# The low half of every second weight block in two mixers, formed by ScalarE and an accumulating DMA in place of a VectorE subtraction

## The chip, the cores and the metric

The kernel runs on one core of one Trainium2 chip. A time is microseconds (us) of device time for one execution of the whole program. The span is the time from the first to the last instruction of the one execution that the hardware profiler recorded.

## The reference

The model is two layers, each of a half-weighted SwiGLU feed-forward, a token mixer and a second feed-forward, with layer norms between; 256 tokens, width 1024, all in float32. The mixer projects `u` by one wide matrix and feeds three branches (a 31-tap causal depthwise convolution, a state-space block, an attention block), whose outputs are gated, merged and projected.

```python
def hybrid_token_mixer(u, w_in, ...):
    proj = jnp.einsum('bsd,de->bse', u, w_in)
    a_in, b_in, c_in, g_in = _split(proj, [A_IN, B_IN, C_IN, GATE_IN])
    y_a = conformer_conv(a_in, ...) @ w_a_out
    y_b = mamba2_ssd(b_in, ...) @ w_b_out
    y_c = nsa_attention(c_in, ...) @ w_c_out
    g = jax.nn.sigmoid(g_in)...
    merged = g[:, :, 0] * y_a + g[:, :, 1] * y_b + g[:, :, 2] * y_c
    return merged @ w_o
```

## The kernel before

**Weights.** The weights come as 128x128 tiles, eight to a unit of 512 KB (`unit`). One DMA on SP's queue loads a unit into a `raw` buffer. For most matrices a float32 product is made of three fast matmuls: ScalarE (ACT) rounds the unit into `whi` (type fp32r), VectorE (DVE) subtracts to get `wlo = raw - whi`, and TensorE (PE) multiplies whi by xh, wlo by xh and whi by xl (`triple`, three lines of code, so three matmuls a tile and 24 a unit). There are 6 buffers for raw, 4 for whi and 4 for wlo, handed out in the order of the units.

**Order.** Every operation is first recorded with a cost, a key (the number of the weight tile at which it is wanted) and its buffers. `schedule` then plays the engines forward with these costs and writes each engine's instructions in the order that comes out. So a changed operation changes the order of all that follows, and the engines then run their lists strictly in order. An operation's `slow` is the time that the planner allows between its end and its users.

**The mixer**, in the order of its keys: `early` and `mix_v` (first projections), `mix_small`, `mix_a` (projection for the convolution, 12 units; the taps themselves are DVE instructions `ca<-ap` and `acc<-ap`, spread with keys up to 670 tiles later), `mix_c` (keys and queries, 16 units), `gates("g2")`, `mix_x` and `attend` (state-space inputs and attention), `merge(0)`, then `mix_z`, `gates("g1")`, `merge(1)` with the `ssd` steps among them, `gates("g0")`, `conv_end`, `merge(2)` (8 units in each of the five) and `mix_out`. At the head of the attention stands `attend_cmp`, run twice: scores `cs` on PE, `st` on ACT, transposes `ct` on PE, a softmax on DVE (`cmx`, `ce`, `csm`), transposes `cp` on PE, `pct` on ACT, and a product `ob`. POOL does small memsets only (`S`, `ap`, `xp`, `kcz`).

Of the kernel before, what the change touches and what calls it, by code (L numbers as in the profile page):

```python
# [13 lines left out]
AF = mybir.ActivationFunctionType  # L14
ALU = mybir.AluOpType
# [78 lines left out]
class Buf:  # L94


    def __init__(self, pool, tag, shape, dt, name, psum):
        self.pool, self.tag, self.shape, self.dt, self.name, self.psum = pool, tag, tuple(shape), dt, name, psum
        self.real = None
        self.live = False  # L100
        self.left = 0
        self.end = 0.0
        self.writes, self.reads = [], []
# [63 lines left out]
def real(x):  # L167
    return x.ap() if isinstance(x, View) else x
# [176 lines left out]
LOW = 0  # L345
# [6 lines left out]
TAIL = (62, 3.0, 44, 30, 4)  # L352
FRONT = 0
MOVE = 2.2
NRAW = 2
ADA0 = 200


class Net(Plan):
    BIG = 11  # L360
    TMP = 12
    RAW = 6
    WHI = 4
    WLO = 4
# [1 line left out]
    def __init__(self, ctx, tc, a):  # L366
        super().__init__()
        self.tc, self.nc, self.a = tc, tc.nc, a
        ctx.enter_context(tc.manual_schedule())
        pool = lambda name, bufs, **k: ctx.enter_context(tc.tile_pool(name=name, bufs=bufs, **k))  # L370
        self.pools = {
            "one": pool("one", 1), "raw": pool("raw", self.RAW), "whi": pool("whi", self.WHI), "wlo": pool("wlo", self.WLO),
            "pad": pool("pad", 1), "b8": pool("big", self.BIG), "t": pool("tmp", self.TMP), "m2": pool("m2", 2), "m3": pool("m3", 3), "m4": pool("m4", 4), "m8": pool("m8", 8),
            "mm": pool("ps", 2, space=PSUM), "x": pool("px", 6, space=PSUM)}
        self.slots = {"raw": self.RAW, "whi": self.WHI, "wlo": self.WLO, "b8": self.BIG, "t": self.TMP, "mm": 2, "x": 6}
        self.pools["pad"].tile([P, 48], F32, name="pad", tag="pad")
        self.nunit = a["ws"].shape[0]
        self.tile_no = 0
        self.keyed = None
        self.mod = {}  # L380
        self.modbuf = {}
        self.splits = {}
        self.last = []
# [140 lines left out]
    def move(self, *pairs):  # L524
# [3 lines left out]

        self.rec("DMA", 0.7 * len(pairs), fn, [p[0] for p in pairs], [p[1] for p in pairs], self.key(), slow=MOVE)

    def unit(self, u, native):
        raw = self.buf(self.pools["raw"], "raw", (P, UNIT * P), F32, "raw")
        base = u * UNIT
        src = self.a["ws"][u]
        self.dma(raw, src, P * UNIT * P * 4, key=base - LEAD)
        self.raw = raw
        if native:
            return
        for n in range(UNIT // SPLIT):
            s = raw[:, n * SPLIT * P:(n + 1) * SPLIT * P]  # L540
            k = base + n * SPLIT - self.EARLY
            hi = self.buf(self.pools["whi"], "whi", (P, SPLIT * P), F32R, "whi")
            lo = self.buf(self.pools["wlo"], "wlo", (P, SPLIT * P), F32R, "wlo")
            self.act(hi, s, AF.Copy, key=k)
            self.tt(lo, s, hi, ALU.subtract, key=k + LOW)
            self.splits[u * (UNIT // SPLIT) + n] = (hi, lo)

    EARLY = 20
# [396 lines left out]
    def mixer(self, l, ada=()):  # L945
        z = self.early(4)
        self.mix_v()
        self.mix_small()
        self.mix_a(l, z)
        self.mix_c(l)  # L950
        self.gates("g2")
        self.mix_x()
        self.attend()
        self.merge(0, self.oh_, self.ol_, th="g2")
        self.ssd0 = self.tile_no
        ada = list(ada)

        def side(i):
            for j in range(COUNT[i] if ada else 0):
                self.ada(*ada.pop(0), self.tile_no + 8 + STEP0 * j)  # L960

        side(0)
        self.mix_z()
        side(1)
        self.gates("g1")
        side(2)
        self.merge(1, *self.ssd(), th="g1")
        side(3)
        self.gates("g0")
        y = self.conv_end()  # L970
        side(4)
        self.merge(2, *y, th="g0")
        self.mix_out(l)

    def mix_v(self):
# [567 lines left out]
    def start(self):  # L1543
# [7 lines left out]
        def raw(k):  # L1551
            n = 2 * FIRST[0] * k - LEAD - FRONT
            raws.append(self.ada_raw(0, k, n))
            self.dma(self.x[:, k], self.a["x"][:, k], P * T * 4, n + 1)

        for k in range(NRAW):
            raw(k)

        def ready(k):
            if k + NRAW < KT:  # L1560
                raw(k + NRAW)
            self.ada(0, 8 + k, -100 + k, k, raws[k])
            self.ts(A[:, k:k + 1], self.mod[0][:, 8 + k:9 + k], 1.0, None, ALU.add, key=-100 + k)
            with self.at(-100 + k):
                self.u_tile(k, self.x[:, k], A[:, k:k + 1], self.mod[0][:, k:k + 1])
            if k == KT - 1:
                for d in range(KT):
                    self.act(self.ha[:, d], self.x[:, d], AF.Copy, scale=ALPHA, key=200)
# [175 lines left out]
```

## Time and profile before

| | |
|---|---|
| median of three runs | 1643.82 us (1637.28 to 1645.85) |
| the profiled execution's own time | 1638.38 us |
| its span | 1636.6 us |
| TensorE busy in the span | 1581.8 us (97%) |
| VectorE busy | 1380.3 us (84%) |
| ScalarE busy | 980.0 us (60%) |
| DMA queue of SP | 350.26 MB, 61.7% of 16 engines' span |

The median is the number that runs are compared by; the span and the stretches below are of the one profiled execution. "Busy" of TensorE includes the overlap of pipelined matmuls, so where it is 100% of a stretch the number of matmuls in that stretch says how fast they went.

### The profile page before, as it was taken

To read this page: it belongs to the slowest core of one execution; us is meant where nothing else is said; L and a number is where in the kernel's file an instruction comes from. 1 tells how busy PE (TensorE), PEld (TensorE's weight loads), DVE (VectorE), ACT (ScalarE), POOL (GpSimd) and SP (SyncE) were. 2 spreads that over 40 slices of the span, in tenths; PEclk is the share of its full clock that TensorE was granted. 3 is DMA by queue.
4 is the path that set the end of the run, shared out by engine and by line. 5 is a ranking of instruction groups with operands and counts; after the bars stand their busy time and mean duration, and the time that the engine had idled before them with its cause. 6 is when DMAs were issued, how large, how long until landed. Compare 5 with 4: busy or idle time off the path is not lost.

```text
span 1636.6 us, 33313 instructions
## 1 busy us (share of the span) xinstructions
PE 1581.8 (97%) x13224; PEld 1503.7 (92%) x13224; DVE 1380.3 (84%) x2675; ACT 980.0 (60%) x1809; POOL 8.3 (1%) x64
## 2 busy tenths in 40 slices
PE   6999999999999999999999999998999999999997
PEld 6999989889988888999989999997999899989996
DVE  7899789999999986899678885999999997776655
ACT  4744585578746466644474445845796567574443
POOL 0000000000000000000000000000000000000000
PEclk9999999999999999999999999999999999999998
DMA  9899665533276555899767985645332544557661
GB/s 375 328 342 406 211 216 179 173 130 100 80 280 206 182 175 188 291 359 361 249 232 272 345 296 174 232 158 172 118 107 91 180 155 165 191 186 234 229 198 46
DMA packets 89883, 352.37 MB, mean 215 GB/s; under 512 B 10368, under 2 KB 13696, under 8 KB 80000
## 3 DMA queue, kind: packets, MB, share of 16 engines
q1 hardware_dynamic: 89728, 350.26, 61.7%
q8 instruction: 103, 1.69, 0.4%
q14 instruction: 52, 0.43, 0.1%
HBM read 343.86 MB, written 1.05 MB: 211 GB/s over the span
## 4 chain that ended last, share of the span: by engine, by line
PE 86%; DVE 7%; DMA 3%; ACT 3%; issue 1%; SPq 0%; ACTq 0%; DVEq 0%
PE mm L573 16%; PE mm L574 16%; PE mm L575 16%; PE mm L451 3%; PE a L451 2%; PE a L589 2%; PE g L573 2%; PE g L574 2%; PE g L575 2%; PE xb L573 2%; DVE wlo L470 2%; PE xb L574 2%; PE xb L575 2%; PE sb L1069 2%; PE ob L1069 1%; DMA ada<-in_ada 1%
## 5 line engine op out<-in xcount | busy, mean ns | idle before, releaser
L507 ACT ACTIVATE whi<-raw 128x1024 fp32r<-128x1024 f32 x470 | 496.7, 1058 | 313.5 <-PE mm L575 147.0
L470 DVE TENSOR_TENSOR wlo<-raw,whi 128x1024 fp32r<-128x1024 f32 x470 | 572.3, 1220 | 130.6 <-ACT whi L507 128.8
L573 PE MATMUL mm<-uh,whi 128*128 128x256 f32 x1392 | 384.9, 277 | 0.9 <-DVE h L470 0.9
L574 PE MATMUL mm<-uh,wlo 128*128 128x256 f32 x1392 | 384.3, 276 | 0.0
L575 PE MATMUL mm<-ul,whi 128*128 128x256 f32 x1392 | 384.3, 276 | 0.0
L573 PEld LDWEIGHTS mm<-uh,whi 128*128 128x128 f32 x1392 | 261.3, 188 | 2.5 <-ACT uh L507 1.2
L575 PEld LDWEIGHTS mm<-ul,whi 128*128 128x128 f32 x1392 | 261.4, 188 | 0.0
L574 PEld LDWEIGHTS mm<-uh,wlo 128*128 128x128 f32 x1392 | 261.3, 188 | 0.1
L489 DVE SCALAR_TENSOR_TENSOR ada<-ada,sc 128x1024 f32<-128x1024 f32 x144 | 173.2, 1219 | 31.7 <-DMA ada<-in_ada 31.4
L573 PE MATMUL mm<-hh,whi 128*128 128x256 f32 x704 | 195.5, 278 | 0.0
L575 PE MATMUL mm<-hl,whi 128*128 128x256 f32 x704 | 194.6, 276 | 0.0
L574 PE MATMUL mm<-hh,wlo 128*128 128x256 f32 x704 | 194.6, 276 | 0.0
L573 PEld LDWEIGHTS mm<-hh,whi 128*128 128x128 f32 x704 | 132.4, 188 | 1.3 <-issue 1.2
L574 PEld LDWEIGHTS mm<-hh,wlo 128*128 128x128 f32 x704 | 132.2, 188 | 0.1
L575 PEld LDWEIGHTS mm<-hl,whi 128*128 128x128 f32 x704 | 132.2, 188 | 0.0
L573 PE MATMUL g<-uh,whi 128*128 128x256 f32 x384 | 113.9, 297 | 0.6 <-DVE g L489 0.6
L489 DVE SCALAR_TENSOR_TENSOR ca<-ap,vec,ca 128x256 f32<-128x256 f32 x240 | 113.9, 476 | 0.2
L574 PE MATMUL g<-uh,wlo 128*128 128x256 f32 x384 | 108.5, 283 | 3.6 <-DVE wlo L470 3.5
L575 PE MATMUL g<-ul,whi 128*128 128x256 f32 x384 | 107.6, 280 | 0.0
L489 DVE SCALAR_TENSOR_TENSOR acc<-ap,vec,acc 128x256 f32<-128x256 f32 x224 | 106.8, 477 | 0.1
L507 ACT ACTIVATE sg<-mm 128x256 f32<-128x256 f32 x76 | 28.9, 382 | 87.8 <-PE mm L575 87.3
L573 PEld LDWEIGHTS g<-uh,whi 128*128 128x128 f32 x384 | 73.5, 191 | 6.9 <-issue 6.2
(343 smaller groups left out, 3582.5 us busy)
## 6 DMA issues: line engine op xcount, KB each, us to landing
raw<-in_ws SPq DMA_DIRECT2D x498, 512.0 KB, 4.3
ada<-in_ada SPq DMA_DIRECT2D x72, 1024.0 KB, 7.9
w<-in_w SPq DMA_DIRECT2D x4, 1024.0 KB, 9.1
pt<-q SPq DMA_DIRECT2D x16, 128.0 KB, 5.3
x<-in_x SPq DMA_DIRECT2D x8, 128.0 KB, 11.1
pt<-kr SPq DMA_DIRECT2D x8, 128.0 KB, 2.1
kh<-kh SPq DMA_DIRECT2D x4, 256.0 KB, 5.1
kl<-kl SPq DMA_DIRECT2D x4, 256.0 KB, 6.1
```

Source lines behind the costliest of these rows:

```text
L451: return self.op("PE", cost, lambda: self.nc.tensor.matmul(real(out), lhsT=real(lhsT), rhs=real(rhs), start=start, stop=stop), [out], [lhs ...
L470: lambda: self.nc.vector.tensor_tensor(real(out), real(a), real(b), op), [out], [a, b], key)
L489: self.nc.vector.scalar_tensor_tensor(real(out), real(a), real(s), real(b), op0, op1, **k)
L507: self.nc.scalar.activation(real(out), real(a), f, **k)
L573: mm(o, lhsT=a, rhs=c, start=start, stop=False)
L574: mm(o, lhsT=b, rhs=c, start=False, stop=False)
L575: mm(o, lhsT=a, rhs=d, start=False, stop=stop)
L589: self.nc.tensor.matmul(o, lhsT=lhsT, rhs=rhs, start=first, stop=False)
L1069: self.nc.tensor.matmul(real(out), lhsT=real(lhsT), rhs=real(rhs), start=start, stop=stop)
```

## The change

In `mix_a`, `mix_c` and from `mix_z` to `merge(2)`, in both mixers, units with an odd number get their low half another way. ACT writes the negated rounded weights into `wlo` (Copy with scale -1), and a DMA issued from POOL's queue adds the raw unit onto it in place (source `raw`, destination `wlo`, both on chip, 512 KB each). The subtraction on DVE falls away for these units: 14 in `mix_a` and `mix_c` and 20 from `mix_z` on, 34 a mixer and 68 in all. The planner is told 1.0 us of POOL and 4.0 us until the result may be used. One of the 12 small temporary buffers of 128x256 is given up, and the room for DMA descriptors in on-chip memory is doubled.

```diff
+ADD = (1.0, 4.0)
...
-    TMP = 12
+    TMP = 11
...
             self.act(hi, s, AF.Copy, key=k)
-            self.tt(lo, s, hi, ALU.subtract, key=k + LOW)
+            if self.added and u % 2:
+                self.act(lo, s, AF.Copy, scale=-1.0, key=k)
+                self.rec("POOL", ADD[0], lambda: self.nc.gpsimd.dma_start(real(lo), real(s), accum_op=ALU.add), [lo],
+                         [lo, s], k, slow=ADD[1])
+            else:
+                self.tt(lo, s, hi, ALU.subtract, key=k + LOW)
...
         self.mix_small()
+        self.added = True
         self.mix_a(l, z)
         self.mix_c(l)
+        self.added = False
         self.gates("g2")
...
         side(0)
+        self.added = True
         self.mix_z()
...
         self.merge(2, *y, th="g0")
+        self.added = False
         self.mix_out(l)
...
-    nc = bacc.Bacc("TRN2", target_bir_lowering=False, num_devices=1, dynamic_dma_scratch_size=1024)
+    nc = bacc.Bacc("TRN2", target_bir_lowering=False, num_devices=1, dynamic_dma_scratch_size=2048)
```

**Place 1, ACT and POOL in `mix_a` and `mix_c` of the first mixer.** ACT before, around the convolution's fifth channel block:

```order
L507 ACTIVATE whi<-raw 128x1024
L507 ACTIVATE ca<-ap_113,cbias,vec 128x256
L507 ACTIVATE acc_3238<-ap_113,vec 128x256
L507 ACTIVATE whi<-raw 128x1024
L507 ACTIVATE th<-mm 128x256
```

ACT now, at the same block:

```order
L509 ACTIVATE whi<-raw 128x1024
L509 ACTIVATE ca<-ap_113,cbias,vec 128x256
L509 ACTIVATE acc_3251<-ap_113,vec 128x256
L509 ACTIVATE whi<-raw 128x1024
L509 ACTIVATE wlo<-raw 128x1024
L509 ACTIVATE ca<-ca 128x256
L509 ACTIVATE th<-mm 128x256
```

Behind every second `whi` there is now a `wlo` of the same size, ahead of what ACT did next.

POOL before, in the same stretch (memsets alone):

```order
L514 MEMSET ap_3415 128x30
L514 MEMSET S 128x16
L514 MEMSET S 64x4
L514 MEMSET kcz 128x1024
L514 MEMSET ap_3954 128x30
```

POOL now:

```order
L549 DMA wlo<-raw 128x1024 x3
L516 MEMSET S 128x16
L516 MEMSET S 64x4
L549 DMA wlo<-raw 128x1024 x2
L516 MEMSET ap_3274 128x30
```

The accumulating DMAs stand among the memsets, and a memset behind one waits until POOL has issued it.

**Place 2, PE and DVE at `attend_cmp` of the first mixer.** PE before, at the second `ct` (g is the projection of `gates("g2")`):

```order
L573 MATMUL g_4221<-uh,whi 128x256
L574 MATMUL g_4221<-uh,wlo 128x256
L575 MATMUL g_4221<-ul,whi 128x256
L451 MATMUL cs<-q,kcz 128x256 x2
L455 MATMUL ct<-cst,st 128x128 x2
L455 MATMUL cp<-cst,ce 128x128 x2
L451 MATMUL ob<-pct_4295,vz_3786 128x256
```

PE now, at the first `cp`:

```order
L580 MATMUL g_4292<-uh,whi 128x256
L581 MATMUL g_4292<-uh,wlo 128x256
L582 MATMUL g_4292<-ul,whi 128x256
L457 MATMUL cp<-cst,ce 128x128 x2
L1080 MATMUL sb<-kh,qs 128x256
L1080 MATMUL sb<-kl,qs 128x256
```

Before, nothing stood between the second `ct` and the first `cp`. Now 36 projection matmuls do.

DVE before, in the softmax between `ct` and `cp`:

```order
L494 TENSOR_REDUCE cmx<-ct 128x16
L470 TENSOR_TENSOR q<-q,pt 128x512
L470 TENSOR_TENSOR ce<-ct,cmx 128x256
L489 SCALAR_TENSOR_TENSOR ca<-ap_107,vec,ca 128x256
L494 TENSOR_REDUCE mx<-sb 128x4
L489 SCALAR_TENSOR_TENSOR qs<-q,qs 64x2x256
L494 TENSOR_REDUCE csm<-ce 128x16
L489 SCALAR_TENSOR_TENSOR acc_3123<-ap_107,vec,acc_3123 128x256
L498 RECIPROCAL csm<-csm 128x16
```

DVE now:

```order
L496 TENSOR_REDUCE cmx<-ct 128x16
L496 TENSOR_REDUCE mx<-sb 128x4
L491 SCALAR_TENSOR_TENSOR qs<-q,qs 64x2x256
L472 TENSOR_TENSOR ce<-ct,cmx 128x256
L472 TENSOR_TENSOR wlo<-raw,whi 128x1024
L491 SCALAR_TENSOR_TENSOR qs<-q,qs 64x2x256
L496 TENSOR_REDUCE csm<-ce 128x16
L496 TENSOR_REDUCE cmx<-ct 128x16
L500 RECIPROCAL csm<-csm 128x16
```

The taps (`ca`, `acc`) have gone from between the softmax steps. Counted over the whole list, DVE has 102 taps of the first mixer behind it when it comes to the first `cmx`; before, it had 74.

## Rows read from the trace of the kernel before

**Rows 1.** The page: span, busy time by engine, and the chain that ended last.

```profile
span 1636.6 us, 33313 instructions
...
PE 1581.8 (97%) x13224; PEld 1503.7 (92%) x13224; DVE 1380.3 (84%) x2675; ACT 980.0 (60%) x1809; POOL 8.3 (1%) x64
...
PE 86%; DVE 7%; DMA 3%; ACT 3%; issue 1%; SPq 0%; ACTq 0%; DVEq 0%
```

**Rows 2.** Busy time in eight stretches: one of a feed-forward, then both mixers'.

```profile
core 0: us, PE busy (x) PEld busy (x) DVE busy (x) ACT busy (x) POOL busy (x), PEclk, DMA share, GB/s
120.00:160.00 40.00, 40.00 (x355) 40.00 (x354) 39.25 (x75) 18.26 (x23) 0.00 (x0) 1.00 1.01 405
238.00:312.00 74.00, 73.50 (x661) 71.89 (x661) 70.75 (x129) 42.00 (x62) 1.42 (x5) 1.00 0.66 197
312.00:340.00 28.00, 21.27 (x139) 18.20 (x138) 27.59 (x54) 12.63 (x27) 0.00 (x0) 0.94 0.34 116
530.00:583.00 53.00, 48.64 (x415) 44.35 (x413) 52.60 (x106) 29.10 (x41) 0.12 (x1) 1.00 0.54 182
583.00:606.00 23.00, 20.88 (x160) 20.05 (x161) 19.47 (x43) 15.91 (x33) 0.00 (x0) 0.93 0.49 155
1050.00:1124.00 74.00, 73.32 (x658) 71.71 (x658) 70.80 (x129) 41.78 (x62) 0.00 (x0) 1.00 0.62 196
1124.00:1152.00 28.00, 21.50 (x139) 18.43 (x138) 27.59 (x54) 12.55 (x26) 0.00 (x0) 0.94 0.33 113
1340.00:1412.00 72.00, 70.83 (x618) 68.24 (x617) 57.91 (x101) 46.99 (x75) 0.00 (x0) 1.00 0.53 175
```

**Rows 3.** TensorE's waits from 312 to 360 us: total, times, longest.

```profile
PE cp L455 <- DVE sm L498: 2.4, 1, 2.4
PE g L574 <- DVE wlo L470: 1.7, 3, 0.9
PE ct L455 <- ACT st L507: 1.0, 1, 1.0
```

**Rows 4.** TensorE's waits from 530 to 606 us.

```profile
PE mm L573 <- ACT yah L507: 2.3, 2, 1.3
PE mm L573 <- DVE g L489: 2.3, 1, 2.3
```

**Rows 5.** Groups of instructions from 238 to 312 us: busy, mean ns, idle before.

```profile
L470 DVE TENSOR_TENSOR wlo<-raw,whi 128x1024 fp32r<-128x1024 f32 x22 | 26.8, 1219 | 0.3
L507 ACT ACTIVATE whi<-raw 128x1024 fp32r<-128x1024 f32 x24 | 25.4, 1056 | 9.5 <-PE kk L575 3.6 <-PE q L575 2.8 <-ACT acc L507 1.9
...
L489 DVE SCALAR_TENSOR_TENSOR ca<-ap,vec,ca 128x256 f32<-128x256 f32 x31 | 14.8, 478 | 0.0
```

**Rows 6.** ScalarE in order of time: start, duration, idle time before.

```profile
249.81 0.38 ACT L507 ACTIVATE th<-mm 128x256 f32<-128x256 f32 x1 [1.61 <-PE mm L575]
250.09 1.05 ACT L507 ACTIVATE whi<-raw 128x1024 fp32r<-128x1024 f32 x1
251.04 0.59 ACT L507 ACTIVATE ca<-ap,cbias,vec 128x256 f32<-128x256 f32 x1
251.53 0.50 ACT L507 ACTIVATE acc<-ap,vec 128x256 f32<-128x256 f32 x1
```

**Rows 7.** Tile raw from 238 to 312 us: its 512 KB loads.

```profile
DMA to landing us min/median/max: 3.3/4.3/7.8
```

**Rows 8.** Tile ada, whole span: its loads of 1024 KB.

```profile
DMA to landing us min/median/max: 4.9/7.9/11.9
```

**Rows 9.** Waits of SP's queue, longest in total.

```profile
SPq L522 <- DVE wlo L470: 840.9, 315, 8.3
```

More of the change, by code (lines that the diff above doesn't have):

```diff
@@ L972, in mixer @@
         self.merge(2, *y, th="g0")
+        self.added = False
         self.mix_out(l)
```

## The prediction

> **What bounds the kernel now.** I began with the page: TensorE is busy for 97% of the span, VectorE for 84%, and the chain that ended last lies on PE for 86% and on DVE for 7% [rows 1]. So TensorE sets the time, and another engine can give time back only where PE stands still. Next I cut the span into stretches to see where that is [rows 2]. In a feed-forward stretch PE issues 355 matmuls in 40 us, 0.113 us each, so a unit of 24 takes 2.70 us; this is the pace of a PE that waits for nothing. In `mix_a` and `mix_c` (238 to 312 and 1050 to 1124 us) PE is idle for only 0.5 and 0.7 us, although DVE is busy for 70.8 of 74. The idle time lies behind them: 28 - 21.27 = 6.7 us at 312 to 340 and 28 - 21.50 = 6.5 us at 1124 to 1152, where `attend_cmp` stands, and 4.4 + 2.1 = 6.5 us at 530 to 606 in the first mixer's end. The second mixer's end has 1.2 us. The list of waits names DVE for most: at the first place `cp` waits 2.4 us for DVE and the g projection 1.7 us for `wlo`, with 1.0 us for ACT [rows 3]; at the other, 2.3 us for DVE's `g` and 2.3 us for ACT's `yah` [rows 4].
>
> The granted clock falls with these stalls: 0.94 over 312 to 340 and 1124 to 1152 and 0.93 over 583 to 606, against 1.00 in the others, so a part of each ran at 1.2 instead of 2.4 GHz [rows 2]. It followed PE standing still. It is worth 0.06 x 28 = 1.7 us at each of the first two and 0.07 x 23 = 1.6 us at the third.
>
> **What the change gives.** It takes 68 subtractions of 1.22 us from DVE [rows 5], 83 us in all, 41 a mixer. In `mix_a` and `mix_c` alone it is 14 x 1.22 = 17 us, in a stretch where PE did not wait; DVE can spend them only on taps. The row list agrees: 28 more taps lie behind DVE at the first `cmx`, 28 x 0.48 = 13 us of work [rows 5] that no longer stands in the softmax. And the planner now has 36 g matmuls, 36 x 0.113 = 4.1 us, between the second `ct` and the first `cp`, where PE stood for 2.4 us before.
>
> - `attend_cmp`, two places: 6.7 + 6.5 us idle and 3.4 us of clock are 16.6 us. A part will stay: the softmax is a chain of short steps over three engines whatever DVE has besides, and the wait for `st` is ACT's. I take two thirds, **11 us**; the bounds are 0 and 16.6.
> - The first mixer's end: 6.5 us idle and 1.6 us of clock are 8.1 us. DVE's share of the two named waits is half, and ACT, which the other half waits for, gets more work there. I take **4 us**; bounds 0 and 8.1.
> - The second mixer's end, 1.2 us: nothing.
>
> **What it costs.** ACT gets 68 roundings of the size of `whi`, 1.06 us each [rows 5], 72 us. In `mix_a` and `mix_c` that is 14 x 1.06 = 15 us on top of 42 of 74, and from 1340 on 12 x 1.06 = 13 on top of 47 of 72 [rows 2], so the work itself lies beside PE's and costs nothing. If that cover were gone, it would be 1.06 us for each unit.
>
> The unknown is the accumulating DMA, of which the trace has none. I call L the time from ACT's end to the moment PE may use `wlo`. What L may be follows from the buffers. With four of each, the buffers of unit u come free when PE ends unit u-4, and units u-3 to u-1 cover what follows: ACT writes `whi` (1.06), then `wlo` (1.06), then L, then PE works through unit u (2.70). The round is 4.82 + L, and at PE's pace it has 4 x 2.70 = 10.8 us. Ahead of `whi` on ACT may stand `th`, `ca` or `acc`, 0.4 to 0.6 us each [rows 6]; I allow 0.4. That leaves L up to **5.6 us**. Beyond it PE waits, once in four units, for the whole excess. The old path, 1.06 + 1.22 us, had more than 5 us to spare.
>
> For L I have two bounds. The add writes 512 KB, as a raw load does: those land 3.3 us after issue at best, 4.3 in the median, 7.8 at worst [rows 7]. It reads two operands, 1 MB, as much as an `ada` load moves: 4.9, 7.9 and 11.9 us, mostly in the crowded feed-forwards [rows 8]. So L lies between 3.3 and 7.9. It moves more than the one and writes less than the other, and the mixers are less crowded; I take 5.5, a little below the middle of 3.3 and 7.9, just inside the room. Since landings scatter, some will be late: I put 0.3 us for each of the 14 rounds of four units in `mix_a` and `mix_c` of both mixers, **4 us**. From 530 to 606 and from 1340 to 1412 some 24 units take 76 and 72 us, so a round has 12.7 and 12.0 us there, and the room for L is over 6.8: nothing.
>
> The Trainium skill has a rule that speaks against this. "Collectives: The Full Stack", in the section on the fold count, says that a reduction in the DMA path is half as fast as a copy, because it reads two sources through the same ring. No row here shows it. By its factor the move of 512 KB, estimated at 1.3 us from the highest rate in the windows, would take 2.6, so L would come 1.3 us above a load's median, 5.6 us, and the sum would stay as it is.
>
> The rest I cost at nothing. A raw buffer of an odd unit now comes free when the add has landed, and SP's next load waits for it as it waited for DVE's `wlo` (840.9 us in total over 315 loads, [rows 9]). Six buffers give 6 x 2.70 = 16.2 us for a load (4.3), both roundings (2.12) and L (5.5), 11.9 in all, with 4.3 to spare; if that is gone, `whi` is late by the excess. On POOL, the memsets of `S` stand behind adds that wait for ACT; POOL was busy for 8.3 us in all [rows 1], and what is late next if an add stalls is DVE's `X`, some us ahead of PE's need. The temporary buffer given up shows in no row: between nothing and what it makes the planner place later.
>
> **Sum.** 1638.4 - 11 - 4 + 4 = 1627.4 us in terms of the profiled execution. The median of the three runs is 5.4 us above that execution, so I predict **1633 us** for the median.
>
> **Rivals.**
>
> *The relief is given back.* The mechanism is right, but L is some 0.5 to 1.5 us over its room, or the softmax's own latency keeps most of the stalls. At L = 6.3 the 14 rounds lose 0.7 to 1.1 us each, 10 to 15 us, as much as is won. Against it: with L near 5.5 the rounds just fit. Time: about 1642.
>
> *The DMA engines fill up, and the kernel is slower.* In `mix_a` and `mix_c` the loads run at 197 GB/s [rows 2]. The adds read 14 x 1.05 MB = 14.7 MB in 74 us, 198 GB/s more, and if both reads count, the sum of 395 GB/s is next to the highest that any stretch shows, 405 at a share of 1.01 [rows 2]. Loads and adds would then queue on each other, and L would go towards an `ada` load's 7.9 us. A round would be 4.82 + 0.4 + 7.9 = 13.1 us, 2.3 over; 14 x 2.3 = 32 us, and 6 x 0.4 + 6 x 1.1 = 9 us in the mixers' ends; with the 15 us won, 26 us slower, about 1670. It decides from L = 6.3 on, and is over 0.5% from about 7. For it: the share is 0.66 before anything is added. Against it: if the write side sets the pace, the adds are 99 GB/s and the sum is 296. "DMA: Bandwidth & Descriptors" of the Trainium skill, section "Issuing engines are not separate DMA queues", says that transfers of all issuers interleave on the same 16 engines; so POOL's queue would be no way round, and no run here shows it yet.
>
> *DVE's time is not wanted.* The taps finish earlier and DVE just idles, while PE's stalls stay because PE's order, not DVE's load, makes them. Then only the 4 us of cost are left: about 1648. The changed order at `cp` speaks against it, so it counts within the first rival's chance.
>
> **How the numbers follow.** Half a per cent, 8.2 us, is about what a measurement of this kernel can tell from no change. The forecast (L up to about 5.7, gain over 8.2 us) has 0.46; its own range is 1619 (everything won, 24.7 us, and no loss) to 1635. The first and third rivals together, within 0.5%, have 0.25; the slower one 0.29. The range for 8 in 10 goes from 1617, the lower end with a little scatter of the runs, to 1664, which leaves out the worst part of the second rival.
>
> **What would show it.** Right: 68 fewer subtractions on DVE; adds landing within about 5.6 us; at `attend_cmp` PE idle for some 2 us in place of 6.6 and the clock back at 1.00; PE's waits for `wlo` in `mix_a` and `mix_c` short and few. Wrong: PE waiting there for a DMA into `wlo` by 1 us or more once in four units, raw loads landing later than 4.3 us in the median, or the idle time at `cp` unchanged. The number I trust least is L.

## The result, and the profile after

The changed kernel is slower: 1694.9 us in the median of 4 runs (1692.8 to 1698.5) against 1640.6 us for the kernel before on the same chip, a ratio of 1.0335 [1.0289, 1.0382], or 54 us. (A pair of numbers in brackets behind a ratio is its 95% interval, here and below.) That is 62 us over the forecast and 31 us over the upper end of the range. The profiled execution of the changed kernel took 1695.6 us with a span of 1693.6 us, 57.0 us longer than before's span [rows 1].

The page of the changed kernel: span, busy time by engine, queues (packets, MB, share of the 16 engines' time), the chain that ended last, the group of POOL's issues, and the issues with KB and median us to landing.

```profile
span 1693.6 us, 33467 instructions
PE 1605.5 (95%) x13224; PEld 1527.3 (90%) x13224; DVE 1311.7 (77%) x2607; ACT 1042.6 (62%) x1877; POOL 67.2 (4%) x132
q1 hardware_dynamic: 89728, 350.26, 58.8%
q0 software_dynamic: 9792, 35.66, 11.5%
PE 63%; DMA 9%; ACT 3%; issue 3%; DVE 3%; SPq 0%; ACTq 0%; POOLq 0%; DVEq 0%
PE mm L581 11%; PE mm L580 11%; PE mm L582 11%; DMA wlo<-raw 6%; PE a L453 2%; PE mm L453 2%; DMA ada<-in_ada 2%; PE g L580 2%; PE xb L580 2%; PE g L581 2%; PE xb L581 2%; PE xb L582 2%; PE g L582 2%; PE sb L1080 2%; PE ob L1080 1%
L549 POOL DMA_DIRECT2D wlo<-raw x68 | 58.9, 866 | 1115.7 <-ACT wlo L509 722.3
raw<-in_ws SPq DMA_DIRECT2D x498, 512.0 KB, 4.5
wlo<-raw POOLq DMA_DIRECT2D x68, 512.0 KB, 5.8
```

The change did what it says: DVE has 68 instructions fewer (2607 for 2675) and 69 us less work, ACT 68 more. But the chain that ended last has gone from 86% PE to 63%, and the new DMAs alone are 6% of it. TensorE's waits name them too (total us, times, longest):

```profile
PE mm L581 <- DMA wlo<-raw: 23.0, 10, 5.6
PE q L581 <- DMA wlo<-raw: 6.9, 2, 4.2
PE g L581 <- DMA wlo<-raw: 3.5, 2, 2.6
PE kk L581 <- DMA wlo<-raw: 3.2, 1, 3.2
PE kc L581 <- DMA wlo<-raw: 0.2, 1, 0.2
```

These are 16 waits, 36.8 us together, all for the low half of an odd unit. Ten of them, 26.0 us, fall into the two stages that are called fronts below.

Since the stages slide against each other, I cut both traces at the same events of the program. Three stages matter. The *front* (`mix_a`, `mix_c`) goes from the first matmul of `v` with the low part of its input to that of `q`; the *attention* from there to `xb`; the *end* from `z` to that of `mgh`. For the second mixer the last such matmuls are taken. In the views by tile of the changed kernel these events are the first and the last time of each row:

```profile
L605 PE MATMUL v<-whi,ul x32: 387/392/395, 220.2 to 1076.7; 128*128 128x512 f32 x32
L582 PE MATMUL q<-ul,whi x128: 276/278/419, 313.2 to 1185.9; 128*128 128x256 f32 x128
L582 PE MATMUL xb<-ul,whi x256: 275/281/287, 383.5 to 1299.8; 128*128 128x256 f32 x128
L582 PE MATMUL z<-ul,whi x128: 275/281/416, 489.8 to 1362.8; 128*128 128x256 f32 x128
L580 PE MATMUL mm<-mgh,whi x128: 276/277/385, 649.6 to 1491.6; 128*128 128x256 f32 x128
```

Busy time in these stages of the kernel before (front, attention and end of the first mixer, then of the second; the columns are those of [rows 2]):

```profile
215.60:289.70 74.10, 73.78 (x627) 70.96 (x626) 70.51 (x145) 49.69 (x85) 1.29 (x4) 1.00 0.62 204
289.70:362.30 72.60, 65.69 (x527) 60.56 (x526) 68.36 (x135) 47.40 (x107) 0.25 (x2) 0.98 0.49 149
468.90:609.60 140.70, 133.76 (x1118) 121.76 (x1117) 132.95 (x269) 85.50 (x156) 0.67 (x3) 0.99 0.58 196
...
1036.40:1124.80 88.40, 87.72 (x782) 86.05 (x781) 83.35 (x161) 54.97 (x87) 0.96 (x1) 1.00 0.67 219
...
1124.80:1248.10 123.30, 116.48 (x982) 107.37 (x981) 115.35 (x258) 98.08 (x271) 1.20 (x12) 0.99 0.33 110
...
1311.20:1434.60 123.40, 122.23 (x1062) 116.11 (x1061) 99.28 (x176) 79.56 (x134) 0.00 (x0) 1.00 0.52 169
```

The same stages of the changed kernel:

```profile
220.20:313.20 93.00, 80.02 (x626) 76.32 (x625) 71.91 (x168) 61.10 (x97) 12.13 (x19) 0.94 0.80 224
313.20:383.50 70.30, 64.09 (x527) 60.06 (x527) 63.07 (x127) 49.58 (x111) 1.97 (x4) 1.00 0.62 177
489.80:649.60 159.80, 142.73 (x1118) 130.02 (x1117) 103.63 (x218) 105.05 (x179) 16.09 (x20) 0.91 0.84 244
...
1076.70:1185.90 109.20, 94.39 (x779) 91.72 (x779) 83.66 (x179) 67.71 (x102) 13.48 (x19) 0.94 0.92 247
...
1185.90:1299.80 113.90, 113.90 (x987) 106.66 (x986) 106.30 (x240) 97.92 (x271) 1.40 (x14) 1.00 0.36 116
...
1362.80:1491.60 128.80, 123.35 (x1063) 115.81 (x1062) 74.30 (x139) 92.47 (x148) 12.96 (x15) 1.00 0.83 231
```

The fronts, where PE had stood still for 0.3 and 0.7 us, are 18.9 and 20.8 us longer. This can be added up from the rows: in the first, PE is idle for 93.00 - 80.02 = 13.0 us, 12.7 more, and the clock of 0.94 is worth 0.06 x 93 = 5.6 us; 18.3 together. In the second it is 14.1 more idle and 6.6 of clock, 20.7. The ends are 19.1 and 5.4 us longer. The attention, where I expected the gain, is 2.3 and 9.4 us shorter. Another 4.6 us lie ahead of the first mixer (last section). The sum is 18.9 + 20.8 + 19.1 + 5.4 - 2.3 - 9.4 + 4.6 = 57.1, the difference of the spans. Of the 26.8 us by which PE's idle time grows in the two fronts, the ten waits for adds are 26.0.

The raw loads land later, too. In the second front, 1036.4 to 1124.8 us before and 1076.7 to 1185.9 after, by the view of tile `raw`:

```profile
DMA to landing us min/median/max: 3.3/4.4/7.3
DMA to landing us min/median/max: 3.4/6.3/13.1
```

How such a wait looks is best seen in order of time (start, duration, idle time before). SP issues two loads of `w`, 1 MB each; POOL issues two adds; PE wants the first add's result and gets it at 254.00; ACT's next `whi` comes after 6.10 us of standing still. The view names no releaser for it, but its buffer comes free only then: PE's last matmul of the waiting unit starts at 258.05 and lasts 0.28 us.

```profile
240.04 0.80 SPq L524 DMA_DIRECT2D w<-in_w  x2
242.44 0.86 POOL L549 DMA_DIRECT2D wlo<-raw  x1 [9.01 <-ACT wlo L509]
247.90 0.86 POOL L549 DMA_DIRECT2D wlo<-raw  x1 [4.33 <-ACT wlo L509]
254.00 0.58 PE L581 MATMUL mm<-uh,wlo 128*128 128x256 f32 x1 [5.61 <-DMA wlo<-raw]
254.38 0.42 PE L582 MATMUL mm<-ul,whi 128*128 128x256 f32 x1
258.41 1.06 ACT L509 ACTIVATE whi<-raw 128x1024 fp32r<-128x1024 f32 x1 [6.10 <-issue]
```

The add took 254.0 - 242.4 = 11.6 us from issue to use. POOL wasn't late: it had waited for ACT, and it issues 0.3 us after ACT's `wlo` has ended. But from 240 to 254 us the DMA engines were full: their share is 1.01 over that stretch, about the highest that a long one shows [rows 2]. After the 5.61 us of waiting PE's matmuls take 0.42 instead of 0.28 us in the records for about 3 us, and the granted clock is 0.50 from 254 to 256 us: the stall brings a stretch at 1.2 GHz with it.

### The profile page after: what moved, and what is told of

Read it like the earlier page. It is cut to its first block, busy times and chain, and to the rows that moved or that the text cites. A ratio compares the mean times of both kernels' runs of the same rounds, so it can differ in the third digit from the quotient of the medians.

```text
span 1693.6 us, 33467 instructions
## 1 busy us (share of the span) xinstructions
PE 1605.5 (95%) x13224; PEld 1527.3 (90%) x13224; DVE 1311.7 (77%) x2607; ACT 1042.6 (62%) x1877; POOL 67.2 (4%) x132
## 3 DMA queue, kind: packets, MB, share of 16 engines
q0 software_dynamic: 9792, 35.66, 11.5%
## 4 chain that ended last, share of the span: by engine, by line
PE 63%; DMA 9%; ACT 3%; issue 3%; DVE 3%; SPq 0%; ACTq 0%; POOLq 0%; DVEq 0%
PE mm L581 11%; PE mm L580 11%; PE mm L582 11%; DMA wlo<-raw 6%; PE a L453 2%; PE mm L453 2%; DMA ada<-in_ada 2%; PE g L580 2%; PE xb L580 2%; PE g L581 2%; PE xb L581 2%; PE xb L582 2%; PE g L582 2%; PE sb L1080 2%; PE ob L1080 1%
## 5 line engine op out<-in xcount | busy, mean ns | idle before, releaser
L472 DVE TENSOR_TENSOR wlo<-raw,whi 128x1024 fp32r<-128x1024 f32 x402 | 490.3, 1222 | 159.5 <-ACT whi L509 157.7
L581 PE MATMUL mm<-uh,wlo 128*128 128x256 f32 x1392 | 390.2, 280 | 15.7 <-DMA wlo<-raw 15.7
L580 PE MATMUL mm<-uh,whi 128*128 128x256 f32 x1392 | 389.8, 280 | 0.9 <-DVE h L472 0.9
L582 PE MATMUL mm<-ul,whi 128*128 128x256 f32 x1392 | 389.4, 280 | 0.0
L581 PEld LDWEIGHTS mm<-uh,wlo 128*128 128x128 f32 x1392 | 264.9, 190 | 16.9 <-DMA wlo<-raw 16.9
L580 PEld LDWEIGHTS mm<-uh,whi 128*128 128x128 f32 x1392 | 265.8, 191 | 2.5 <-ACT uh L509 1.2
L582 PEld LDWEIGHTS mm<-ul,whi 128*128 128x128 f32 x1392 | 265.1, 190 | 0.0
L580 PE MATMUL g<-uh,whi 128*128 128x256 f32 x384 | 114.9, 299 | 0.0
L549 POOL DMA_DIRECT2D wlo<-raw x68 | 58.9, 866 | 1115.7 <-ACT wlo L509 722.3
```

Source lines behind the costliest of these rows:

```text
L472: lambda: self.nc.vector.tensor_tensor(real(out), real(a), real(b), op), [out], [a, b], key)
L549: self.rec("POOL", ADD[0], lambda: self.nc.gpsimd.dma_start(real(lo), real(s), accum_op=ALU.add), [lo], [lo, s], k, slow=ADD[1])
L580: mm(o, lhsT=a, rhs=c, start=start, stop=False)
L581: mm(o, lhsT=b, rhs=c, start=False, stop=False)
L582: mm(o, lhsT=a, rhs=d, start=False, stop=stop)
```

## Experiments

My first theory was the second rival: the adds fill the DMA engines, so they and the raw loads land late, and PE waits for the low halves. The other theories were that ACT's extra work or the new order of the instructions costs the time, that the planner's figure of 4.0 us places the adds too late, that the ring of four buffers is too short, and that the temporary buffer given up matters. In each comparison the kernel before ran on the same chip.

The lengths of the stages tell more than the whole time. In us, from the same rows by tile as above:

| kernel | front 1, 2 | attention 1, 2 | end 1, 2 |
|---|---|---|---|
| before | 74.1, 88.4 | 72.6, 123.3 | 140.7, 123.4 |
| after | 93.0, 109.2 | 70.3, 113.9 | 159.8, 128.8 |
| no add | 75.8, 89.3 | 65.7, 114.9 | 140.0, 125.7 |
| copy | 85.6, 100.3 | 70.3, 114.0 | 150.5, 127.7 |
| every fourth unit | 81.4, 99.4 | 67.2, 116.9 | 147.1, 125.7 |
| front only | 92.9, 108.8 | 72.4, 113.9 | 136.6, 122.3 |
| ends only | 74.0, 88.1 | 72.8, 122.3 | 156.2, 130.1 |
| POOL subtracts | 81.9, 97.9 | 65.9, 115.4 | 150.1, 123.9 |
| after, five `wlo` | 87.3, 100.0 | 72.8, 120.8 | 155.0, 127.7 |
| before, five `wlo` | 74.1, 88.0 | 75.5, 125.2 | 140.7, 123.7 |
| after, no split `ada` | 92.2, 108.9 | 70.8, 114.2 | 145.4, 132.9 |
| before, no split `ada` | 74.0, 88.2 | 72.2, 124.0 | 130.2, 122.2 |

**1. The add is not issued.** Everything else stays, the order and ACT's second rounding with it.

```diff
-                self.rec("POOL", ADD[0], lambda: self.nc.gpsimd.dma_start(real(lo), real(s), accum_op=ALU.add), [lo],
+                self.rec("POOL", ADD[0], lambda: None, [lo],
```

> Order, buffers and ScalarE work of the changed kernel, but the accumulating DMA isn't issued; the low half is left as the negated rounded weights. Lateness theory (the adds land after the ring of four buffers needs them, and TensorE waits): the loss goes and VectorE's relief shows, 1620 to 1632 us against 1640 before. Order theory (ScalarE's 72 us more and the new order cost the time): stays at 1685 or above. Crowding theory (the adds slow the raw loads): as the lateness theory, with raw loads back at 4.3 us in the median.

Measured: 1629.9 us against 1639.0 for the kernel before, ratio 0.9936 [0.9913, 0.9959]. The median landing of the raw loads is back at 4.3 us. No wait of PE for a `wlo` is left in the fronts, and PE is busy through them again, at a clock of 1.00:

```profile
220.50:296.30 75.80, 73.83 (x626) 70.79 (x625) 71.00 (x168) 60.25 (x97) 1.42 (x5) 1.00 0.60 199
...
1036.10:1125.40 89.30, 87.57 (x778) 85.90 (x777) 80.65 (x176) 67.32 (x102) 0.96 (x1) 1.00 0.66 214
```

So the whole loss, and more, is the DMA itself and the waiting for it: 1694.9 - 1629.9 = 65 us. ACT's 72 us of work and the new order together cost only a little: the fronts stay 1.7 and 0.9 us and the second end 2.3 us longer than before. The run also gives the worth of the relief: attention is 6.9 and 8.4 us shorter than before, 15 us in all. It is only a bound for what a cheaper way to form the low half could reach, not such a way. In the profiled executions the spans are 62.5 us apart. Of these, 40.1 us are PE idle ((1693.6 - 1605.5) - (1631.1 - 1583.1)) and 20.7 us are clock (0.018 x 1693.6 - 0.006 x 1631.1, by the mean granted clocks of 0.982 and 0.994).

**2. A copy in place of the add.** The same buffers, bytes written and waits, but one source.

```diff
-                self.rec("POOL", ADD[0], lambda: self.nc.gpsimd.dma_start(real(lo), real(s), accum_op=ALU.add), [lo],
+                self.rec("POOL", ADD[0], lambda: self.nc.gpsimd.dma_start(real(lo), real(s)), [lo],
```

> The changed kernel with a plain copy of the raw unit into the low half from the same queue at the same place, not an addition; the low half is then the raw weights. If the second operand that an addition reads is the price: landing falls from 5.8 by about 1.3 us to 4.5, the time to about 1660 us. If the queue and the fixed part of a transfer are the price: landing within 0.4 us of 5.8, time 1685 to 1695. Order theory: no change, 1690 or above, whatever the landing.

Measured: 1664.5 us, 1.0146 [1.0097, 1.0196]. From its page, the share of the 16 engines' time that the DMAs took, and their landing by the view of tile `wlo`:

```profile
q0 software_dynamic: 9792, 35.66, 6.0%
```

```profile
DMA to landing us min/median/max: 2.8/4.9/10.3
```

The page counts the same packets and bytes as for the add, but half the time. An add takes 0.115 x 1693.6 / 68 = 2.86 us of all 16 engines, a copy 0.060 x 1665.4 / 68 = 1.47, a factor of 1.95. An add's figure doesn't depend on how crowded the engines are: with half as many adds (run 5) it is 0.058 x 1657.9 / 34 = 2.83 us. The minimum to landing is 2.8 us for the copy and 4.5 for the add. The copy costs 35 us over no DMA and the second operand another 30. So about half the price is there at half the engines' time. The copy also lands sooner, so this run doesn't tell the engines' time from the time of the single transfer. The Trainium skill's rule in "Collectives: The Full Stack", section on the fold count, gives a reduction two reads per write and half the rate of a copy; the trace agrees with that factor, here for an add within on-chip memory.

**3. The planner is told 6.5 us** instead of 4.0 until the result may be used, which is nearer to what was measured.

```diff
-ADD = (1.0, 4.0)
+ADD = (1.0, 6.5)
```

> The changed kernel with the planner told 6.5 in place of 4.0 us from the add's issue to its use. Lateness theory: the ring itself is short, so the planner can only put other work in front; time 1670 to 1695. If the loss were a planner's error alone: back to 1645 or below. Order theory: any time, no tie to the waits for adds.

Measured: 1688.8 us, 1.0298 [1.0255, 1.0341]. The order changes, the fronts stay at 90.5 and 111.4 us and the waits at 27.7 us. So the loss is no mere error of the planner's figure: with a figure near the measured landing, another order comes out and nearly all of the loss stays.

**4. The layout alone:** the kernel before with the change's buffers.

```diff
-    TMP = 12
+    TMP = 11
...
-    nc = bacc.Bacc("TRN2", target_bir_lowering=False, num_devices=1, dynamic_dma_scratch_size=1024)
+    nc = bacc.Bacc("TRN2", target_bir_lowering=False, num_devices=1, dynamic_dma_scratch_size=2048)
```

> The kernel before with 11 temporary buffers and the doubled descriptor room, no adds. Lateness theory: within 0.5% of before, 1632 to 1650 us. Order theory, or a price of the memory layout: 1650 or above. It also tells whether the slower matmul pace that the changed kernel's profile shows at 60 to 170 us (87 or 88 matmuls in 10 us against 90 or 91) comes with the layout: if so it shows here too.

Measured over 10 runs: 1639.6 us, 0.9999 [0.9977, 1.0022]. The buffer given up and the room for descriptors cost nothing.

**5. Half as many adds.**

```diff
-            if self.added and u % 2:
+            if self.added and u % 4 == 1:
```

> Adds for every fourth unit only, 34 in all. Lateness theory, ring alone: the late slot comes round once in four units as before, so most of the loss stays, 1665 to 1685 us. Crowding theory (adds and loads queue on each other): half the adds leave room, landing falls to 5.0 us or less in the median and the time to 1635 to 1655.

Measured: 1656.0 us, 1.0117 [1.0093, 1.0141]. The adds land faster, and few waits remain:

```profile
DMA to landing us min/median/max: 4.5/4.9/11.0
```

```profile
PE mm L581 <- DMA wlo<-raw: 12.8, 4, 4.7
PE g L581 <- DMA wlo<-raw: 0.6, 2, 0.4
```

At half the rate the median falls from 5.8 to 4.9 us, below the room of 5.6, so the adds' landing does depend on how many there are. The time is 1 us above what I had expected of full engines, and 9 below what I had expected of a short ring alone. But the kernel is still 20 us slower than before. The longest add still takes 11.0 us, and four waits make up nearly all of the time that PE waits for adds. A median below the room is not enough.

**6 and 7. Adds in the fronts only, and in the ends only.**

```diff
         side(0)
-        self.added = True
         self.mix_z()
```

> Adds in mix_a and mix_c only, 28 in all, none from mix_z on. From the stages of the changed kernel's trace (first v to first xb: 16.6 us longer in the first mixer, 11.4 in the second) 28 us over before: 1660 to 1675 if the stages' losses stand by themselves; below 1655 if the ends' loss was the larger part.

```diff
         self.mix_small()
-        self.added = True
         self.mix_a(l, z)
```

> Adds from mix_z to the second merge only, 40 in all. From the trace (first z to first mgh 19 us longer in the first mixer, 5.4 in the second) 24 us over before: 1655 to 1670. With the crowding theory nearly all of it in the first mixer, where the ada loads of 1 MB run beside the adds; with the ring alone about even between the mixers.

Measured: front only 1665.9 us, 1.0183 [1.0146, 1.0221]; ends only 1666.9 us, 1.0182 [1.0151, 1.0212]. The losses stay in the stage that has the adds (see the table): 18.8 and 20.4 us in the fronts with the one, 15.5 and 6.7 in the ends with the other. Over the kernel before the two cost 30 and 31 us, 60 together against the 54 of the change. Without adds in the ends the first of these is even 4.1 us shorter than before. So the ends, which I had put at nothing, lose 22 us against the 39 of the fronts, and as much in the whole time, since with adds in the fronts alone 9.6 us come back in the attentions.

**8. POOL subtracts itself,** for every fourth unit, with no DMA and no second rounding.

```diff
+ADD = (2.6, 0)
...
+            if self.added and u % 4 == 1:
+                self.rec("POOL", ADD[0], lambda: self.nc.gpsimd.tensor_tensor(real(lo), real(s), real(hi), ALU.subtract), [lo],
+                         [hi, s], k)
```

> No DMA and no extra ScalarE work: POOL itself subtracts for every fourth unit of the same stretches (34 subtractions), 12 temporary buffers and the old descriptor room. If relief of VectorE alone decides: 1630 to 1640 us. If POOL and VectorE hinder each other's operands, or POOL takes over 5 us: 1640 to 1670, with VectorE's subtractions and taps longer than 1.22 and 0.48 us.

Measured: 1662.2 us, 1.0156 [1.0121, 1.0191]. POOL's group of subtractions, then VectorE in order of time and POOL's subtraction beside it:

```profile
L548 POOL TENSOR_TENSOR wlo<-raw,whi 128x1024 fp32r<-128x1024 f32 x34 | 94.6, 2782 | 1027.8 <-ACT whi L509 982.1
```

```profile
248.93 2.52 POOL L548 TENSOR_TENSOR wlo<-raw,whi 128x1024 fp32r<-128x1024 f32 x1 [8.85 <-ACT whi L509]
...
249.10 2.63 DVE L491 SCALAR_TENSOR_TENSOR ca<-ap,vec,ca 128x256 f32<-128x256 f32 x1
251.66 0.48 DVE L491 SCALAR_TENSOR_TENSOR acc<-ap,vec,acc 128x256 f32<-128x256 f32 x1
```

One tap takes 2.63 us instead of 0.48, as long as POOL's subtraction beside it. So an instruction that gives 1.22 us back to DVE blocks it here for 2.15. Over the whole run DVE is busy for 1406.2 us against 1380.3 before, although it has 34 subtractions fewer. The Trainium skill says in "SBUF — State Buffer", section "Who interferes with whom", that a VectorE instruction with two inputs from that memory contends with a GpSimd instruction that reads it, over a pair of ports held by one of the two at a time; this trace agrees. In this form it is no way out.

**9 and 10. Five `wlo` buffers** (and five of `raw`, for the room), in the changed kernel and in the kernel before with the change's other buffers.

```diff
-    RAW = 6
+    RAW = 5
...
-    WLO = 4
+    WLO = 5
```

> The changed kernel with five buffers for the low half and five for raw (six before). Ring theory: the low half may be started a unit, 2.7 us, earlier, so the waits for adds mostly go: 1675 us or less, 20 below the changed kernel. Crowding theory: the adds land no sooner and with one raw buffer less the loads come later: 1685 us or above.

> The control of the run above: the kernel before with the same buffers (five low, five raw, 11 temporary) and no adds. Both theories: 1635 to 1650 us; what it is over 1640 is the price of the raw buffer and is to be taken off the run above.

Measured: 1684.2 us, 1.0255 [1.0207, 1.0303], and 1650.5 us over 9 runs, 1.005 [1.0021, 1.0079]. The first lies between what I had expected of a short ring and of full engines. With the same buffers the change costs 34 us instead of 54. With a fifth buffer ACT writes `wlo` ahead of its unit's `whi`, not behind it, since it no longer waits for the same end on PE: in the run the two start at 264.13 and 265.19 us,

```profile
264.13 1.04 ACT L509 ACTIVATE wlo<-raw 128x1024 fp32r<-128x1024 f32 x1
265.19 1.06 ACT L509 ACTIVATE whi<-raw 128x1024 fp32r<-128x1024 f32 x1
```

while in the changed kernel `whi` starts at 264.07 and `wlo` at 265.03. Set against its `whi`, the add thus starts 2 us sooner, there and in most units behind it. The fronts lose 13.2 and 12.0 us in place of 18.9 and 20.8, although the median landing has risen to 7.1 us. So the ring's length is a part of the cause, a third of the fronts' loss here; the rest stays with two more us of room. The raw buffer given up has a price of its own here: in the second front ACT's `whi` waits 8.3 us for raw loads, which it does in neither front of the changed kernel.

**11 and 12. No split loads of `ada` in these stretches,** after and before, to see whether it is these 1 MB loads that make the adds late.

```diff
-SPLITA = 48
+SPLITA = 64
```

> The changed kernel with the eight ada loads of the first mixer's end moved back into the first feed-forward. To be read against the control below. Crowding theory: the first mixer's end (first z to first mgh) loses 6 us or less to its control instead of 19, landing there 5.5 us in the median without the 10 to 12 us ones, and the two kernels differ by 35 to 45 us. Ring theory: they differ by 50 or more, as before and after do.

> The control: the kernel before with the same move of the ada loads. The feed-forward is already at a DMA share of 1.0 at 120 to 160 us, so it should pay for the 8 MB: 1645 to 1665 us under both theories.

Measured: 1689.8 us, 1.0301 [1.0255, 1.0348], and 1639.9 us over 10 runs, 0.9985 [0.9963, 1.0008]. I had expected the second to be slower; it isn't. The difference stays at 50 us. The first mixer's end, which has no `ada` load now, still loses 15.2 us to its control, where I had expected 6 or less, though PE's waits for adds there fall from 9.1 to 3.9 us. The median landing of all adds is 6.3 us and PE's waits for them rise in total, from 36.8 to 39.2 us; the longest rows:

```profile
PE mm L581 <- DMA wlo<-raw: 28.0, 13, 6.8
PE q L581 <- DMA wlo<-raw: 6.4, 2, 3.3
```

That form of my theory falls: the `ada` loads may make some adds late in that end, but most of the loss doesn't rest on them. What is left in the fronts are the adds, the raw loads and four loads of `w`.

## Why the prediction was wrong

**Bounds and relief: right.** TensorE was the bound, and DVE's load did cost time at `attend_cmp`. I put 11 us there; without the add the attentions are 15.3 us shorter, PE idles there for 2.1 and 0.4 us in place of 6.9 and 6.8 by the same cut, and the clock is 1.00 in place of 0.98 and 0.99. In the changed kernel 11.7 us of this arrive.

**The first mixer's end: wrong by 3 us.** Without the add this stage is 140.0 us long against 140.7: it wins 0.7 us with 31 us less work of DVE, where I had put 4. Of the waits in [rows 4] the one for DVE's `g` is gone, but the one for ACT's `yah` has grown from 2.3 to 3.7 us, and the clock is 0.96 in place of 0.99. So the relief came and was given back, in part by ACT, whose extra work I had put at nothing. In the second end it is the same: PE waits 3.5 us for ACT's `g` in place of 1.2. The whole relief, net of all this, is 9 us without the add; I had 15.

**The cost: this step failed.** I wrote that L is 5.5 us, "just inside the room" of 5.6, that late ones cost 0.3 us a round, and 4 us in all. The DMA cost 65 us. The room itself was about right: the 16 adds that PE waited for took 5.7 to 11.7 us from issue to landing, and the two nearest to 5.6, with 5.7 and 6.5, cost only 0.2 and 0.6 us. The term for the late ones was wrong: PE waited 26.0 us in the fronts, with nine waits over 1 us in the 14 rounds. Four things stand in its place.

- L's median wasn't far off: 5.8 us over all adds. But in the fronts it is 6.3 us in the first mixer and 7.1 in the second, above the room; and single adds scatter from 4.5 to 11.7 us. With the 5.61 us wait shown above a single late add costs more than I gave all seven rounds of a front. Half the rate brought the median to 4.9 and still left 12.8 us in four waits. The slow adds make the loss, and I had priced the typical one.
- I counted the adds' work on a single transfer and not on the 16 engines. 14 adds of 2.86 us need 40 us of all engines in each front. In the second front the engines worked for 0.92 x 109.2 = 100.5 us, against 0.67 x 88.4 = 59.2 before: 41 more. The 100.5 us alone are longer than the 88.4 us that the stage had, so there was no place left in which the adds could have been hidden. In the first it is 0.80 x 93.0 = 74 us for a stage of 74.1. The share of 0.66 in [rows 2] had stood there beforehand: it is 49 us of work in 74, and with the 40 of the adds 89. The Trainium skill's factor of two, from "Collectives: The Full Stack", section on the fold count, which I weighed, would have given the estimate of 14 x 2.6 = 36 us for the adds, 85 in all. I used it for L alone.
- The raw loads come from the same 16 engines and land later as well: in the second front their median goes from 4.4 to 6.3 us, the longest from 7.3 to 13.1. "DMA: Bandwidth & Descriptors" in the Trainium skill, section "Issuing engines are not separate DMA queues", says that transfers run on the same 16 engines and interleave, whichever engine issued them; the trace agrees. In the fronts this cost nothing that shows: no view of the changed kernel names a wait of ACT for a raw load there.
- I gave the stalls no price in clock. The change takes 12.7 us of idle and 5.6 of clock in the first front, and 20.7 us of clock in all against run 1. About a third of those 62.5 us is not waiting but matmuls at 1.2 GHz behind a wait.

**The ends: "nothing" was wrong.** A round of 12.7 and 12.0 us had room for L of 6.8 and more by the mean pace. But adds come there with a median of 7.5 us from 489 to 560 us (5.9 over the whole stage), and the first end lost 19.1 us. PE idles there 10.1 us more, with 9.1 us of waits for adds, and is busy 9.0 us longer with the same 1118 matmuls, at a clock of 0.91 in place of 0.99.

**The rival that came true** is the second, the DMA engines that fill up, with the sign that I gave and, as far as the runs tell, the mechanism. Its price of 26 us is half of the 54. It lacked the clock and put 9 us on the ends, which cost 24.5. Its own idle time for the fronts, 32 us, is close to the 26.8 measured. Its chance of 0.29 was too low: the row that should have raised it, the share of 0.66, stood in [rows 2]. I named it as an argument, but set its price by bytes per second and not by time.

**What stays open.** How the loss divides between the ring's length and full engines isn't settled: the fifth buffer had to be paid for with a raw buffer, and the landings grew with it. Nor is it shown what the latest adds stand behind. The `ada` loads are not the main cause. The four `w` loads of 1 MB, two in each front, are a rival that no run moved: in the changed kernel four of the seven slowest adds (9.8 to 11.5 us) were issued while one or two of them were under way, and in run 11 the four slowest of all (9.6 to 11.6 us). Two of the ten waits in the fronts, 9.1 of the 26.0 us, are for such adds. No kernel here that forms all low halves was faster than before; the best with adds took 1656 us.

## What to carry to other kernels

Work that is moved from an engine to a DMA has two prices: its latency, and its time on the DMA engines, which all loads share. Take the second from the share column and add it to the stage's own, with an accumulating transfer counted as two copies (1.95 here), before looking at the first; and size the ring of buffers for the slowest transfer, not the median. A relief that is real (15 us in the attentions and 9 in all here, shown by leaving the DMA out) is no argument as long as the engine that takes the work over stands in the way of the one that bounds the kernel. A stall of TensorE can also cost the clock after it, 20.7 of 62.5 us here.

## What the runs showed that I had not expected

- An accumulating DMA of 512 KB within on-chip memory took 2.86 us of all 16 engines, a plain copy 1.47; 4.5 and 2.8 us from issue to landing at least. The page's MB and GB/s count both alike, so a share of 0.92 goes with only 247 GB/s, while a feed-forward reached 405 at 1.01 [rows 2].
- A tap on DVE took 2.63 us instead of 0.48 while POOL subtracted beside it.
- In the stretch from 60 to 170 us, ahead of the first mixer, PE issued 929 matmuls in the profiled execution of the changed kernel and 971 in that of before, at a granted clock of 1.00 in both. The 42 matmuls are 42 x 0.113 = 4.7 us, as much as the 4.6 us ahead of the first mixer. The profiles of runs 1, 9 and 10 show 927 to 933 as well, those of runs 2 to 8 962 to 973, with and without the change. There is one profile of each kernel, so whether this belongs to the kernel or to the single execution stays open, and with it whether these 4.6 us are the change's.
